# Splitting a block of 640 keys as 384 + 256 columns instead of 512 + 128 in three attention loops

## The chip, the cores and the metric

The kernel runs on one core of one Trainium2 chip. The metric is the device time of one execution in microseconds (us), given as the median of the timed runs. The engines are called as the profile calls them: PE (TensorE, matrix products), PEld (its weight loads), DVE (VectorE), ACT (ScalarE), POOL (GpSimd), SP (the engine that issues most transfers).

## The reference

One layer of a decoder on 1024 positions of width 1024: a half-step SwiGLU, then two attentions side by side that are gated and added, then a second half-step SwiGLU. What matters here are three products with all keys up to a query's own position:

```
# sparse attention: an indexer scores every key, the best 256 are kept
dots  = einsum('bthd,bsd->bths', q_idx, k_idx)          # 8 heads of 64
score = einsum('bths,bth->bts', relu(dots), w_idx)
_, idx = top_k(where(causal, score, -inf), 256)
logits = einsum('bthd,btkd->bthk', q_a, k_a[idx]) * 64 ** -0.5
p = softmax(logits)                                     # then p @ v_a[idx]

# stick-breaking attention, 8 heads of 64
z = einsum('bthd,bshd->bhts', q_b, k_b) * 64 ** -0.5
log_a = log_sigmoid(z) + (reverse cumulative sum of log_sigmoid(-z), strictly causal)
a = exp(log_a)                                          # then a @ v_b
```

All inputs are float32. Queries are handled in 8 blocks of 128; block i may look at the first (i + 1) * 128 keys.

## The kernel before

**Numbers.** Products in full precision are made from parts: an operand is split into a high part in the fast float32 form of PE and the remainder (the low part), and three products (high by high, high by low, low by high) are added up in one accumulator bank; `mm3` at line 310 is that. In the three loops of this change the query's two parts are stacked in the 128 rows of the weight operand, so two products do: one with the high part of the keys, one with the low part.

**The course of the kernel.** The first feed-forward and the projection of the latent queries take up to about 690 us of the profile. Then come two stages in which many small jobs are interleaved by a planner: "index" (queries and keys of the indexer, index scores, and the projections of the second attention as filler work) and "attend" (stick-breaking attention, the threshold of the top 256, sparse attention, more projections and the output products). From about 1410 us on the output projection and the second feed-forward run.

**The planner.** In the two middle stages nothing is left to the scheduler of the language: inside `tc.manual_schedule` (line 1058) the engines run their instructions in the order in which Python writes them. That order is chosen by the class `Weave` (lines 95 to 244). Every job is a generator that yields the engine and the tiles it needs next; `Weave.run` picks, step by step, the job that can begin first by a model of time, and at equal times the one of lower rank. The model gives each instruction a price by engine and width (`cost`, line 113). For PE it is

```
return 0.01 + max(outs[0].free_size(), 240) / 2350, 0.0
```

so the width of a matmul moves the model's clock of PE, and through it every later choice in both stages. `late` and the ranks decide only between jobs that can begin at the same time. The filler jobs on PE (`fillers` at 1232, which writes tiles `psf` and `psvb`, and `outputs` at 2145, which writes `psob` and `psoa`) have the last ranks and take the gaps.

**The three loops.** Each takes the key range of one query block in pieces of at most 512 columns, since one accumulator bank holds 512 float32 values a row. For each piece it takes a bank from one ring of three (`ubank`, line 1091), writes two matmuls and spawns a job that empties the bank.

- `indexer` (line 1681): blocks 5, 4, 2, 7, 6, 3, eight heads each; matmuls at 1695 and 1696 into `psdot`. `dot_out` applies the rectifier on ACT (1665) into one of two tiles `relu` and adds the weighted result to the score `u` on DVE (1670 for the first head, 1672 for the others), head after head for each piece.
- `sticks` (line 1761): for each head blocks 4 to 7, then 0 to 3; matmuls at 1778 and 1779 into `psz`; `sigmoids` on ACT (1753), then one running product over the whole row on DVE (1759).
- `logits` (line 1959): blocks 5, 4, 1, 0, 7, 6, 3, 2, eight heads each; matmuls at 1978 and 1979 into `psL`; `logit_out` on DVE (1938) adds the mask of the selected keys and takes the row's maximum for each piece, `soft` joins the maxima and applies the exponential on ACT.

A last piece of 128 keys is computed as 256 columns (`max(w, 256)` at 1694 and 1774, `max(n_, 256)` at 1976), and the job that empties the bank reads only the first 128 of them. That holds for blocks 0 (128 keys) and 4 (640 keys = 512 + 128).

Of the kernel before, what the change touches and what calls it, by code (L numbers as in the profile page):

```python
# [94 lines left out]
class Weave:  # L95
# [89 lines left out]
    def mark(self, name, *needs):  # L185
        self.marks[name] = needs

    def give(self, *tiles):
        for t in tiles:
            self.held[t.tensor.name] -= 1  # L190
# [19 lines left out]
    def spawn(self, gen, rank=1, own=None):  # L210
        s = Stream(gen, rank, own or self.own)
        self.streams.append(s)
        self.step(s)
        return s
# [33 lines left out]
def trunk(ctx, tc, x, positions, g_ffn1, w1_gate, w1_up, w1_down, g_mix, w_in, g_cq, w_uq_a, w_q_idx,  # L248
# [17 lines left out]
    def ht(name, dt=F32R):  # L266
        return hpool[-1].tile([P, 1024], dt, tag="h", name=name, bufs=16)

    def sm(name, n=1, dt=F32, bufs=4):
        return small.tile([P, n], dt, name=name, bufs=bufs)  # L270
# [39 lines left out]
    def mm3(ps, ah, al, bh, bl, first, last):  # L310

        nc.tensor.matmul(ps, ah, bh, start=first, stop=False)  # L312
        nc.tensor.matmul(ps, ah, bl, start=False, stop=False)  # L313
        nc.tensor.matmul(ps, al, bh, start=False, stop=last)  # L314

    def in_turn(*sources):

        order = [f for n in range(max(n for f, n in sources)) for f, m in sources if n < m]
        at = [0]

        def tile_(name):
            at[0] += 1
            return order[(at[0] - 1) % len(order)](name)

        return tile_
# [59 lines left out]
    class Right:  # L385
# [72 lines left out]
        def keep(self, copies, eng=None):  # L458

            for t, (ps, g) in copies:  # L460
                if eng is nc.vector:
                    nc.vector.tensor_scalar(t, ps, g, None, op0=ALU.mult)
                else:
                    nc.scalar.activation(t, ps, AF.Copy, scale=g)
# [374 lines left out]
    def ring(pool):  # L839

        op = in_turn((wt, 4), (lambda name: pool.tile([P, 1024], F32R, tag="r", name=name, bufs=NR), NR))
        raw = in_turn((rawt, 2), (lambda name: pool.tile([P, 1024], F32, tag="raw", name=name, bufs=2), 2))
        return op, raw
# [7 lines left out]
    with tc.tile_pool(name="ring1", bufs=1) as rpool, tc.tile_pool(name="s1", bufs=1) as spool, tc.tile_pool(name="ps1", bufs=1, space=PSUM) as psum:  # L851
# [3 lines left out]
        with tc.tile_pool(name="t1", bufs=1, side="right") as tpool, tc.tile_pool(name="c1", bufs=1) as cpool:  # L855
# [52 lines left out]
            first = [[load(w, q, f"a{e}r0") for q in range(2)] for e, w in enumerate((w1_gate, w1_up))]  # L908
# [149 lines left out]
    with fp as fpool, psm as psum, tc.manual_schedule(  # L1058
# [157 lines left out]
        def late(rank):  # L1216

            return rank if "sparse" in weave.marks and "gates" not in weave.marks else None
# [442 lines left out]
        def dot_out(ps, i, h, c0, w, acc, before):  # L1661
            yield ACT, ps, relus
            rt = relus("relu")
            r = rt[:, 0:w]
            nc.scalar.activation(r, ps[:, 0:w], AF.Relu)  # L1665
            give(ps)
            yield DVE, rt, before
            wv, ac = WI[:, i, h:h + 1], acc[:, c0:c0 + w]
            if h == 0:
                nc.vector.tensor_scalar(ac, r, wv, None, op0=ALU.mult)  # L1670
            else:
                nc.vector.scalar_tensor_tensor(ac, r, wv, ac, op0=ALU.mult, op1=ALU.add)  # L1672
            give(rt)

        def score_out(i, acc, outs):
            nk = (i + 1) * P
            yield POOL, *outs, acc
            nc.gpsimd.affine_select(acc[:, i * P:nk], acc[:, i * P:nk], pattern=[[-1, P]], compare_op=ALU.is_ge,
                                    fill=LOW, base=0, channel_multiplier=1)

        def indexer():

            for i in order:
                yield PE, "kidx", f"qi{i}"
                nk = (i + 1) * P
                acc = keep(f"u{i}", f"u{i}", 1, shape=(P, nk))
                outs = {}
                for h in range(H):
                    for c0 in range(0, nk, 512):
                        w = min(512, nk - c0)  # L1690
                        yield PE, ubank
                        ps = ubank("psdot")
                        lh = QI[i][:, h * P:(h + 1) * P]
                        x = max(w, 256)
                        nc.tensor.matmul(ps[:, 0:x], lh, KX["h"][:, c0:c0 + x], start=True, stop=False)
                        nc.tensor.matmul(ps[:, 0:x], lh, KX["l"][:, c0:c0 + x], start=False, stop=True)
                        outs[c0] = spawn(dot_out(ps, i, h, c0, w, acc, outs.get(c0)))
                give(QI[i])
                score[i] = acc
                mark(f"score{i}", spawn(score_out(i, acc, list(outs.values()))))  # L1700
# [28 lines left out]
        for n, g in enumerate((latents(), keys(), indexer(), index_queries())):  # L1729
            spawn(g, n)  # L1730
# [20 lines left out]
        def sigmoids(zp, left, c0, w):  # L1751
            yield ACT, zp
            nc.scalar.activation(left[:, c0:c0 + w], zp[:, 0:w], AF.Sigmoid, scale=-1.0)  # L1753
            give(zp)

        def stick(outs, left, nk):
            yield DVE, *outs, left, hidden
            back, ones = left[:, 0:nk][:, ::-1], hidden[:, S - nk:S][:, ::-1]
            nc.vector.tensor_tensor_scan(back, back, ones, 1.0, op0=ALU.mult, op1=ALU.max)  # L1759

        def sticks():

            n, ends = 0, []
            for h, c in work:
                yield PE, f"hq{h}"
                qs, kh, kl = HQ[h]
                for i in range(4 * c, 4 * c + 4):
                    nk = (i + 1) * P
                    yield PE, arings[c]
                    left = arings[c]("left")  # L1770
                    outs = []
                    for c0 in range(0, nk, 512):
                        w = min(512, nk - c0)
                        x = max(w, 256)
                        yield PE, ubank
                        zp = ubank("psz")
                        lq = qs[:, i * P:(i + 1) * P]
                        nc.tensor.matmul(zp[:, 0:x], lq, kh[:, c0:c0 + x], start=True, stop=False)
                        nc.tensor.matmul(zp[:, 0:x], lq, kl[:, c0:c0 + x], start=False, stop=True)
                        outs.append(spawn(sigmoids(zp, left, c0, w)))  # L1780
                    A[n] = left
                    ends.append(spawn(stick(outs, left, nk)))
                    mark(f"s{n}", ends[-1], left)
                    n += 1
                if not c:
                    give(qs, kh, kl)
            mark("sparse", *ends)
# [147 lines left out]
        def logit_out(lp, e, bias, c0, n_, m):  # L1935
            yield DVE, lp
            c = slice(c0, c0 + n_)
            nc.vector.tensor_tensor_reduce(e[:, c], lp[:, 0:n_], bias[:, c], 1.0, LOW, op0=ALU.add, op1=ALU.max,  # L1938
                                           accum_out=m)
            give(lp, bias)  # L1940
# [18 lines left out]
        def logits():  # L1959
            n = 0  # L1960
            yield PE, "sparse", "ka2", "warm"
            kah, kal = KV[:2]
            for b, i in enumerate(blocks):
                nk = (i + 1) * P
                yield PE, f"qa{b}", f"bias{b}"
                QS, bias = QA[b], BIAS[b]
                for h in range(H):
                    rings = [arings[1], lefts] + ([here["e"]] if "e" in here else [])
                    yield PE, rings, late(2)
                    ring = min(rings, key=lambda r: weave.when((r,), PE))  # L1970
                    e, mx, outs = ring("e"), sm("mx", 2, F32, 8), []
                    for g, c0 in enumerate(range(0, nk, 512)):
                        yield PE, ubank, late(2)
                        lp = ubank("psL")
                        n_ = min(512, nk - c0)
                        w = max(n_, 256)
                        lh = QS[:, h * P:(h + 1) * P]
                        nc.tensor.matmul(lp[:, 0:w], lh, kah[:, c0:c0 + w], start=True, stop=False)
                        nc.tensor.matmul(lp[:, 0:w], lh, kal[:, c0:c0 + w], start=False, stop=True)  # L1979
                        outs.append(spawn(logit_out(lp, e, bias, c0, n_, mx[:, g:g + 1])))  # L1980
                    E[n] = e
                    mark(f"p{n}", spawn(soft(n, e, nk, mx, outs)), e)
                    n += 1
                give(QS)
# [182 lines left out]
        first = [feed().parts for n in range(2)]  # L2167
# [6 lines left out]
    with ctxf, tc.tile_pool(name="ring2", bufs=1) as rpool, tc.tile_pool(name="ps6", bufs=1, space=PSUM) as psum:  # L2174
        op, raw = ring(rpool)
        bank = banks(psum, fpsum)
        with tc.tile_pool(name="m0", bufs=1) as mpool:
            M0 = []
            for d in range(0, ND, 2):
                wh, wl = first.pop(0) if first else wcols(w_o_a, d * P, 2 * P, 0, 4, f"woa{d}")  # L2180
                for e in range(2):
                    r = slice((d + e) * P, (d + e + 1) * P)
                    g = ht("gate", F32)
# [150 lines left out]
```

## Time and profile before

| What | Value |
|---|---|
| Median of 3 timed runs | 2137.19 us (2136.37 to 2138.1) |
| Span of the profiled execution | 2135.7 us |
| Busy: PE, PEld, DVE | 2122.0, 1779.9, 1512.9 us |
| Busy: ACT, POOL | 1065.8, 910.1 us |
| Matmuls | 10284 |
| Chain of work that ended last, by engine | PE 93%, DVE 3%, DMA 2%, ACT 1%, issue 1% |

The profile shows one execution; its span runs from the first instruction to the last. Its own time is that span; the median of the timed runs lies 1.5 us above it. A matmul's duration in the rows contains its way through the array, and the next one begins before it ends: what a matmul takes of PE is the distance from its start to the next start.

### The profile page before, as it was taken

The page shows a single profiled execution, that of the slowest core. Times are in us where ns is not written, and L with a number is a line of the kernel's source. Part 1 is how long each engine was busy: PE and PEld are TensorE (multiplying, and loading weights), DVE is VectorE, ACT ScalarE, POOL GpSimd, SP SyncE. Part 2 cuts the span into 40 slices and gives each one's busy share as a digit, 9 for nine tenths or more (in the row PEclk, how much of TensorE's full clock was granted, in tenths as well). Part 3 has the DMA queues.
Part 4 walks back from the last instruction along what each step waited for, and adds up shares of the span by engine and source line. Part 5 has one row for each costly group of instructions (what it writes and reads, how often), then busy time and mean ns, then how long its engine had stood idle before and what let it go on. Part 6 is the DMA issues. An engine that isn't in the chain of part 4 may idle for free.

```text
span 2135.7 us, 30056 instructions
## 1 busy us (share of the span) xinstructions
PE 2122.0 (99%) x10284; PEld 1779.9 (83%) x10284; DVE 1512.9 (71%) x2587; ACT 1065.8 (50%) x2005; POOL 910.1 (43%) x732
## 2 busy tenths in 40 slices
PE   9999999999999999999999999999999999999999
PEld 7888888888889988888888888888888888888887
DVE  7776767688875498898886777754765646578675
ACT  6343343334455357888777686534432222324443
POOL 6654555522355434322311432354664555542233
PEclk9999999999999999999999999999999999999999
DMA  5587867497685342776744534574142333359655
GB/s 149 148 252 212 260 199 239 153 335 245 209 228 165 103 148 85 241 198 163 198 135 162 193 127 149 172 250 142 55 131 92 118 94 117 101 187 333 216 176 188
DMA packets 277578, 377.33 MB, mean 177 GB/s; under 512 B 39840, under 2 KB 165440, under 8 KB 277424
## 3 DMA queue, kind: packets, MB, share of 16 engines
q1 hardware_dynamic: 265392, 337.61, 51.1%
q0 software_dynamic: 12032, 37.79, 4.8%
q8 instruction: 81, 1.33, 0.3%
q14 instruction: 73, 0.60, 0.1%
HBM read 258.38 MB, written 116.95 MB: 176 GB/s over the span
## 4 chain that ended last, share of the span: by engine, by line
PE 93%; DVE 3%; DMA 2%; ACT 1%; issue 1%; POOL 0%; SPq 0%; ACTq 0%; POOLq 0%; DVEq 0%
PE p L769 6%; PE p L770 6%; PE p L768 6%; PE psf L312 4%; PE psf L314 4%; PE psf L313 4%; PE pd L529 3%; PE pd L531 3%; PE pc L529 3%; PE pd L530 3%; PE pa L529 3%; PE pa L531 3%; PE pa L530 3%; PE pc L531 3%; PE pc L530 3%; PE pb L531 2%
## 5 line engine op out<-in xcount | busy, mean ns | idle before, releaser
L1315 ACT ACTIVATE junka<-u,cand,sig 128x768 bf16<-128x768 f32 (+2 forms) x124 | 134.2, 1082 | 3.6 <-DVE cand L1307 2.3
L891 ACT ACTIVATE swh<-swr 128x512 fp32r<-128x512 f32 x48 | 30.2, 630 | 121.4 <-PE pc L531 48.5
L1759 DVE TENSOR_TENSOR_SCAN left<-left,hidden 128x640 f32<-128x640 f32 (+3 forms) x64 | 87.3, 1382 | 0.9 <-ACT left L1753 0.6
L892 DVE TENSOR_TENSOR swr<-swr,swh 128x512 f32<-128x512 f32 x48 | 43.2, 901 | 51.8 <-ACT swh L891 51.7
L672 ACT ACTIVATE b0u<-b0u 128x512 f32<-128x512 f32 x20 | 12.6, 632 | 99.8 <-DVE b0u L552 84.4
L1938 DVE CUSTOM_DVE_ANT_0 e<-psL,bias 128x512 f32<-128x512 f32 (+3 forms) x96 | 49.3, 551 | 16.9 <-PE psL L1979 12.2
L1817 DVE TENSOR_TENSOR pt<-pspT,pt 128x512 fp32r<-128x512 f32 x72 | 46.7, 684 | 18.3 <-ACT pt L1811 18.2
L1814 DVE SCALAR_TENSOR_TENSOR pt<-pstT,pt 128x512 fp32r<-128x512 f32 (+1 forms) x96 | 51.0, 546 | 12.1 <-ACT pt L1811 11.7
L1811 ACT ACTIVATE pt<-pstT 128x512 fp32r<-128x512 f32 (+1 forms) x96 | 46.1, 493 | 22.4 <-PE pstT L1871 19.9
L1950 ACT ACTIVATE e<-e,nm 128x768 f32<-128x768 f32 (+7 forms) x64 | 49.2, 774 | 8.7 <-DVE nm L1945 8.7
L1811 ACT ACTIVATE pt<-pspT 128x512 fp32r<-128x512 f32 x72 | 39.7, 596 | 26.2 <-PE pspT L2033 26.1
L1665 ACT ACTIVATE relu<-psdot 128x512 f32<-128x512 f32 (+1 forms) x80 | 40.5, 520 | 23.9 <-DVE u L1672 13.3
L769 PE MATMUL p<-aT,aS 128*128 128x512 f32 x132 | 51.5, 390 | 0.8 <-DVE aT L382 0.8
L769 PE MATMUL p<-bT,bS 128*128 128x512 f32 x132 | 51.3, 389 | 0.0
L770 PE MATMUL p<-aT,aS 128*128 128x512 f32 x132 | 50.7, 389 | 0.0
L770 PE MATMUL p<-bT,bS 128*128 128x512 f32 x132 | 50.7, 389 | 0.0
L1672 DVE SCALAR_TENSOR_TENSOR u<-relu,WI,u 128x512 f32<-128x512 f32 (+1 forms) x70 | 48.1, 705 | 3.4 <-ACT relu L1665 2.5
L1229 POOL DMA_DIRECT2D gd<-evg x32 | 18.2, 569 | 75.7 <-ACT evg L1224 56.2
L768 PE MATMUL p<-bT,bS 128*128 128x512 f32 x132 | 47.0, 389 | 0.0
L1871 PE MATMUL pstT<-ident,left 128*128 128x128 f32 x288 | 46.0, 272 | 0.0
L768 PE MATMUL p<-aT,aS 128*128 128x512 f32 x132 | 44.9, 389 | 0.0
L381 ACT ACTIVATE bT<-bt 128x512 fp32r<-128x512 f32 x44 | 26.6, 626 | 35.9 <-PE p L770 30.8
(3051 smaller groups left out, 8191.2 us busy)
## 6 DMA issues: line engine op xcount, KB each, us to landing
aw<-in_w_down_dram SPq DMA_DIRECT2D x33, 512.0 KB, 4.6
bw<-in_w_down_dram SPq DMA_DIRECT2D x33, 512.0 KB, 4.6
swr<-in_w_in_dram SPq DMA_DIRECT2D x48, 256.0 KB, 6.1
a0r<-in_w_gate_dram SPq DMA_DIRECT2D x22, 512.0 KB, 8.6
a1r<-in_w_up_dram SPq DMA_DIRECT2D x22, 512.0 KB, 8.5
b0r<-in_w_gate_dram SPq DMA_DIRECT2D x22, 512.0 KB, 4.1
b1r<-in_w_up_dram SPq DMA_DIRECT2D x22, 512.0 KB, 3.9
x<-in_x_dram SPq DMA_DIRECT2D x16, 512.0 KB, 5.9
```

Of the source, the lines that this page charges most:

```text
L312: nc.tensor.matmul(ps, ah, bh, start=first, stop=False)
L313: nc.tensor.matmul(ps, ah, bl, start=False, stop=False)
L314: nc.tensor.matmul(ps, al, bh, start=False, stop=last)
L529: nc.tensor.matmul(ps, a[:, c], b[k][:, HI], start=start and k == 0, stop=False, skip_group_check=True)
L530: nc.tensor.matmul(ps, a[:, c], b[k][:, LO], start=False, stop=False, skip_group_check=True)
L531: ins = nc.tensor.matmul(ps, a[:, l], b[k][:, HI], start=False, stop=k == 3, skip_group_check=True)
L768: nc.tensor.matmul(ps[q][m], S[:, h], T[:, HI], start=p == 0, stop=False)
L769: nc.tensor.matmul(ps[q][m], S[:, h], T[:, LO], start=False, stop=False)
L770: nc.tensor.matmul(ps[q][m], S[:, l], T[:, HI], start=False, stop=p == last)
L1315: nc.scalar.activation(junks[1][:, 0:(i + 1) * P], score[i], AF.Sign, scale=sig[:, b:b + 1], bias=cand.bitcast(F32)[:, b:b + 1], accum_out ...
L1759: nc.vector.tensor_tensor_scan(back, back, ones, 1.0, op0=ALU.mult, op1=ALU.max)
L1811: nc.scalar.activation(pt[:, off:512], tp[:, off:512], AF.Copy, bias=-less)
```

## The change

A new helper cuts a key range into pieces, and the three loops use it in place of `range(0, nk, 512)`:

```
+    def chunks(nk):
+        first = 512 if nk - 512 >= 256 or nk <= 512 else nk - 256
+        return [(c0, min(first, nk) if not c0 else nk - first) for c0 in range(0, nk, first)]
...
-                    for c0 in range(0, nk, 512):
-                        w = min(512, nk - c0)
+                    for c0, w in chunks(nk):
                         yield PE, ubank
                         ps = ubank("psdot")
...
-                    for c0 in range(0, nk, 512):
-                        w = min(512, nk - c0)
+                    for c0, w in chunks(nk):
                         x = max(w, 256)
                         yield PE, ubank
                         zp = ubank("psz")
...
-                    for g, c0 in enumerate(range(0, nk, 512)):
+                    for g, (c0, n_) in enumerate(chunks(nk)):
                         yield PE, ubank, late(2)
                         lp = ubank("psL")
-                        n_ = min(512, nk - c0)
                         w = max(n_, 256)
```

Up to 512 keys there is one piece as before; 768, 896 and 1024 keys give 512 + 256, 512 + 384 and 512 + 512 as before. Only block 4 differs: its 640 keys are 384 + 256 instead of 512 + 128, and the second piece needs no padding: its matmuls cover keys 384 to 639 where they covered 512 to 767. The number of pieces, banks and instructions written for a block stays the same.

## Prediction

> **What bounds the kernel now.** I read the page first: busy time by engine and the granted clock.
>
> ```profile
> span 2135.7 us, 30056 instructions
> ...
> PE 2122.0 (99%) x10284; PEld 1779.9 (83%) x10284; DVE 1512.9 (71%) x2587; ACT 1065.8 (50%) x2005; POOL 910.1 (43%) x732
> ...
> PEclk9999999999999999999999999999999999999999
> ```
>
> PE is busy 99% at a full clock. But that share overlaps the matmuls, so I looked next at the stretches in which the change acts, by the view of windows (columns after the length: busy us and instructions of PE, PEld, DVE, ACT, POOL, then the granted clock and the DMA load). The three later windows are the index stage, stick-breaking with what runs beside it, and sparse attention.
>
> ```profile
> core 0: us, PE busy (x) PEld busy (x) DVE busy (x) ACT busy (x) POOL busy (x), PEclk, DMA share, GB/s
> 10.00:15.00 5.00, 4.72 (x23) 4.25 (x22) 4.34 (x8) 3.14 (x6) 1.83 (x2) 0.50 1.22 294
> 690.00:900.00 210.00, 207.35 (x1221) 182.40 (x1220) 161.90 (x349) 129.96 (x260) 86.54 (x106) 1.00 0.42 140
> 900.00:1150.00 250.00, 249.78 (x1314) 209.93 (x1313) 209.73 (x427) 203.67 (x420) 59.44 (x81) 1.00 0.64 181
> 1150.00:1410.00 260.00, 259.17 (x1358) 218.15 (x1357) 194.91 (x551) 165.47 (x328) 84.23 (x79) 1.00 0.47 155
> ```
>
> PE's idle time is 210 - 207.35 = 2.65 us, 250 - 249.78 = 0.22 us and 260 - 259.17 = 0.83 us: 3.7 us in 720. The second busiest engine, DVE, has 77% (161.9 of 210), 84% (209.7 of 250) and 75% (194.9 of 260). Third, the waits of PE in that stretch (total us, times, longest):
>
> ```profile
> PE psdot L1695 <- ACT relu L1665: 1.4, 3, 1.0
> PE pscqt L1486 <- DMA cqn<-cqd: 1.1, 1, 1.1
> PE psout L313 <- POOL wout000l L301: 0.4, 1, 0.4
> PE pso L2015 <- DVE pt L1817: 0.3, 1, 0.3
> PE psz L1778 <- ACT left L1753: 0.2, 1, 0.2
> ```
>
> These five make 3.4 of the 3.7 us. Of the loops that change, the indexer waits three times for its bank to be emptied by ACT, `sticks` once, `logits` not at all in this list. So in both stages PE is the bound, filler products take the gaps, and a microsecond less on PE is a microsecond less of the stage, as long as the planner's order stays about as good.
>
> **What a column costs on PE.** Last, single starts in the timeline (start, duration). Three neighbouring places give three widths:
>
> ```profile
> 1341.27 0.33 PE L1979 MATMUL psL<-kkl,qs 128*128 128x384 f32 x1
> 1341.44 0.34 PE L1978 MATMUL psL<-kkh,qs 128*128 128x384 f32 x1
> 1341.62 0.34 PE L1979 MATMUL psL<-kkl,qs 128*128 128x384 f32 x1
> 1341.80 0.35 PE L1978 MATMUL psL<-kkh,qs 128*128 128x384 f32 x1
> ```
>
> ```profile
> 1176.71 0.28 PE L1978 MATMUL psL<-kkh,qs 128*128 128x256 f32 x1
> 1176.82 0.28 PE L1979 MATMUL psL<-kkl,qs 128*128 128x256 f32 x1
> 1176.94 0.40 PE L1978 MATMUL psL<-kkh,qs 128*128 128x512 f32 x1
> ...
> 1178.09 0.39 PE L312 MATMUL psf<-mhi,wg6h 128*128 128x512 f32 x1
> ...
> 1179.90 0.39 PE L314 MATMUL psf<-mhi,wg6l 128*128 128x512 f32 x1
> ```
>
> The last two rows are the first and the ninth of nine matmuls of 512 columns in a row: eight distances in 1179.90 - 1178.09 = 1.81 us, 0.226 us each. The 384 columns take (1341.80 - 1341.27) / 3 = 0.177 us, and the 256 columns (1176.94 - 1176.71) / 2 = 0.115 us. The starts are rounded to 0.01 us, so the three-step distance is good to about 0.003 us.
>
> **The change, part by part.** *PE, the only term.* Block 4 alone changes. In each of three loops it has 8 heads, and each head two passes (high and low part of the keys): 3 x 8 x 2 = 48 times a pair of matmuls of 512 + 256 columns becomes one of 384 + 256. The second matmul of the pair keeps its width; it only loses its padding and covers other keys. One matmul per pair goes from 512 to 384 columns: 0.226 - 0.177 = 0.049 us. 48 x 0.049 = 2.35 us, taken as **2.4 us off PE**: 0.8 us each in the indexer, in `sticks` and in `logits`.
>
> The bounds come from other rows for the same step: durations by form (busy us, mean ns), and the weight load that goes with each matmul.
>
> ```profile
> L1696 PE MATMUL psdot<-kil,qsi 128*128 128x512 f32 x48 | 18.9, 393 | 0.0
> L1696 PE MATMUL psdot<-kil,qsi 128*128 128x384 f32 x16 | 5.4, 338 | 0.0
> L1778 PE MATMUL psz<-kkh,qs 128*128 128x512 f32 x48 | 20.1, 419 | 0.0
> L1778 PE MATMUL psz<-kkh,qs 128*128 128x384 f32 x16 | 5.7, 353 | 0.0
> L1979 PE MATMUL psL<-kkl,qs 128*128 128x512 f32 x48 | 18.9, 393 | 0.0
> L1979 PE MATMUL psL<-kkl,qs 128*128 128x384 f32 x16 | 5.4, 338 | 0.0
> L1979 PEld LDWEIGHTS psL<-kkl,qs 128*128 128x128 f32 x96 | 18.2, 189 | 1.7
> ```
>
> The durations shrink by 393 - 338 = 55 ns in the low passes and 419 - 353 = 66 ns in the high pass of `sticks`; 48 x 0.060 = 2.9 us is the upper end. The lower end would be a weight load that sets the pace: 189 ns are more than 177 ns, and 0.226 - 0.189 = 0.037 us a step gives 1.8 us. I take 2.4, since matmuls of 256 columns start 0.115 us apart with the same loads, which therefore lie beside the products.
>
> A page of the Trainium skill speaks for less. "TensorE: Matmul & The Clock Gate", section "Back-to-back issue gap", gives a sustained 81 ns a matmul at 128 columns and 131 ns at 512 where each matmul comes with its own weight load. By that slope 128 columns would be worth an estimated 17 ns, and the change 0.8 us. This trace does not agree: 226 ns at 512 columns in such a stream, with 177 ns at 384 and 115 ns at 256 on one line, and the measurement decides.
>
> *ACT and DVE, which empty the banks.* Before, 512 and 128 columns; after, 384 and 256. The same number of instructions, and all four forms are in the trace:
>
> ```profile
> L1753 ACT ACTIVATE left<-psz 128x512 f32<-128x512 f32 x48 | 28.7, 604 | 0.7 <-PE psz L1779 0.6
> L1753 ACT ACTIVATE left<-psz 128x384 f32<-128x384 f32 x16 | 8.0, 501 | 0.1
> L1753 ACT ACTIVATE left<-psz 128x256 f32<-128x256 f32 x16 | 6.3, 393 | 0.2 <-PE psz L1779 0.2
> L1753 ACT ACTIVATE left<-psz 128x128 f32<-128x128 f32 x16 | 4.5, 279 | 0.0
> L1938 DVE CUSTOM_DVE_ANT_0 e<-psL,bias 128x512 f32<-128x512 f32 x48 | 32.0, 684 | 9.1 <-PE psL L1979 7.6 <-issue 1.5
> L1938 DVE CUSTOM_DVE_ANT_0 e<-psL,bias 128x384 f32<-128x384 f32 x16 | 8.6, 550 | 0.9 <-PE psL L1979 0.9
> L1938 DVE CUSTOM_DVE_ANT_0 e<-psL,bias 128x256 f32<-128x256 f32 x16 | 6.5, 418 | 5.8 <-POOL o L2104 3.2 <-PE psL L1979 2.6
> L1938 DVE CUSTOM_DVE_ANT_0 e<-psL,bias 128x128 f32<-128x128 f32 x16 | 4.2, 284 | 1.0 <-PE psL L1979 1.0
> ```
>
> ACT in `sticks`: 604 + 279 = 883 ns becomes 501 + 393 = 894 ns. DVE in `logits`: 684 + 284 = 968 ns becomes 550 + 418 = 968 ns. Eight heads each: 0.1 us at most, on engines with at least 16% of each stretch free. Taken as nothing; PE's filler products hide it. If that cover were gone, the second bank of a head would come free 393 - 279 = 0.11 us later after its matmul and the first 604 - 501 = 0.10 us earlier: eight times 0.1 us in each loop at worst, 2.4 us over 24 heads, and as likely a gain as a loss.
>
> No transfer is added, dropped or moved past a queue, no wait is added, and the ring of three banks turns as often as before.
>
> *The planner.* Its model prices the narrower matmul at 0.01 + 384 / 2350 = 0.173 us instead of 0.228 us, 0.055 us less, close to the 0.049 us of the trace. So the plan stays as true as it was, but its clock of PE runs ahead from the first head of block 4 in the indexer, and two candidates that were nearly level can swap. From there to the end of sparse attention (about 620 us, over 3000 matmuls) the order may differ in detail, with the same work in it. What changes are the waits where plan and chip part. Bounds from the trace: all 3.7 us of PE's idle time in the stretch can go at best; at worst new ones come, of the size of the largest there is now. Its rows:
>
> ```profile
> 828.09 0.28 PE L314 MATMUL psvb<-wvb11h,mlo 128*128 128x256 f32 x1
> 829.38 0.50 PE L1695 MATMUL psdot<-kih,qsi 128*128 128x512 f32 x1 [1.02 <-ACT relu L1665]
> ```
>
> From start to start that is 1.29 us where a 256-column matmul takes 0.115 us: 1.17 us lost. I take zero for the reordering, between -3.7 us and some +9 us (eight such waits), since I have no reason for either sign.
>
> **Sum.** -2.4 us on a span of 2135.7 us gives 2133.3 us. The median of the timed runs lies 2137.19 - 2135.7 = 1.5 us above the span, and nothing in the change touches that difference: 2137.19 - 2.4 = **2134.8 us**, 0.11% less. About 0.2% (4.3 us) is what a measurement of this kernel can tell from no change, so the forecast is one of no change that can be told.
>
> **Rivals.**
>
> *The reordering also loses waits* (2131 us). All five waits above stem from places where the plan meant the bank, the transfer or the operand to be ready. A new order may miss them: at best 2137.19 - 2.4 - 3.7 = 2131.1 us. For it: the three `psdot` waits lie in the stage where the order first changes, and the first piece's bank is free 0.10 us sooner. Against it: the waits for `pscqt` and `psout` (1.5 us) lie before block 4's first head and after the last of its work, so the change reaches only 2.2 us of the 3.7.
>
> *The reordering adds waits in the index stage* (2144 us, slower). The mechanism: between two heads of the indexer the PE stands in line behind a `psdot` matmul whose bank ACT has not emptied, and ACT waits for a `relu` tile that DVE frees; every filler product is queued behind that matmul and none can pass it. The place is 740 to 860 us. The price is 1.17 us a wait. It decides for "slower" from the sixth new wait on (6 x 1.17 = 7.0, less 2.4 = 4.6 us); eight make 9.4 - 2.4 = 7.0 us, 2144.2 us. For it: idle time is largest there (2.65 of 210 us). Against it: six to eight are many where three are now, ACT and DVE get no more work, and DVE is at 77%. The clock could raise that price: in the window of 10 to 15 us, just after the kernel's first waits, it was granted at 0.50, and five microseconds at half speed are 2.5 us of work lost. The Trainium skill ("TensorE: Matmul & The Clock Gate", section "Why this matters for your kernels") warns of gaps over about 3 us between bursts of matmuls; the largest single wait in the stretch here is 1.17 us, so this trace shows no case of it there.
>
> *The narrower matmul does not free PE* (2137.2 us). If the start of the next product were set by something else than columns, say by its weight load, at most 1.8 us would be left, or nothing. Against it stand the three distances above, which follow the width. By the slope of the Trainium skill quoted above ("TensorE: Matmul & The Clock Gate", "Back-to-back issue gap") the estimate would be 2136.4 us, which lies in this case.
>
> **How the numbers follow.** The forecast has 0.55: the sum holds, with the waits changed by less than 1.9 us either way. Fewer waits have 0.22; I count 0.18 of that beyond 4.3 us of gain, the rest within. More waits have 0.18, of which 0.14 lie over 4.3 us of loss. No effect of the narrower matmul has 0.05. So: faster by over 0.2% 0.18, within 0.2% 0.55 + 0.04 + 0.04 + 0.05 = 0.68, slower by over 0.2% 0.14. The range goes from 2130.8 us (2.9 + 3.5 us of gain: the upper end of the term and nearly all the idle time) to 2141.0 us (five and a half new waits of 1.17 us, less 2.4), and leaves some 0.05 below and 0.12 above it.
>
> **What the profile of the changed kernel would show.** Right: of the rows of 512 columns for `psdot`, `psz` and `psL` 40 instead of 48 are left on each line, 24 instead of 16 of 384 columns; 128-column rows of lines 1665, 1753 and 1938 lose eight and 256-column rows gain eight; the second feed-forward starts, and its first product lies, about 2.4 us earlier, 0.8 us of it in each of the three windows; PE's idle time between 690 and 1410 us stays near 3.7 us. Wrong in the size: consecutive 384-column starts 0.19 us or more apart. Wrong in the planner's part: PE's idle time in that stretch moves by more than 2 us, with new rows among its waits, above all for `psdot`.

## The result, and the profile after

The changed kernel takes 2148.9 us (median of 5 runs, 2147.73 to 2150.88); the kernel before took 2137.74 us beside it (5 runs, 2136.37 to 2141.63). The ratio is 1.0052, with a 95% interval of 1.004 to 1.0064: 11.2 us slower by the medians, where 2.4 us less was forecast.

The page of the changed kernel, with PE's row of the 40 slices (53.7 us each):

```profile
span 2147.1 us, 30062 instructions
...
PE 2121.3 (99%) x10284; PEld 1779.4 (83%) x10284; DVE 1511.8 (70%) x2587; ACT 1064.9 (50%) x2005; POOL 917.9 (43%) x732
...
PE   9999999999999999999999899999999999999999
```

The span grew by 2147.1 - 2135.7 = 11.4 us while PE's busy time fell by 0.7 us. So PE got no more work (POOL shows 7.8 us more for the same 732 instructions, but it is busy for 43% of the span only); PE stands still somewhere, and the slice with the 8 (1181 to 1235 us) says about where. The windows of the three stages narrow it down (same columns as in the prediction):

```profile
690.00:900.00 210.00, 204.79 (x1208) 179.56 (x1206) 162.34 (x339) 125.74 (x252) 88.19 (x106) 1.00 0.44 144
900.00:1150.00 250.00, 249.19 (x1315) 210.71 (x1316) 212.40 (x443) 207.94 (x430) 61.97 (x81) 1.00 0.62 177
1150.00:1410.00 260.00, 250.63 (x1316) 211.31 (x1314) 178.08 (x535) 159.30 (x318) 78.07 (x76) 0.99 0.45 150
```

PE is idle for 5.2, 0.8 and 9.4 us where it was idle for 2.65, 0.22 and 0.83 us, and in the last stage the granted clock is no longer 1.00. PE's waits in this stretch (total us, times, longest) name the place:

```profile
PE pso L2015 <- ACT pt L1814: 8.6, 3, 7.0
PE psz L1781 <- ACT left L1757: 1.7, 1, 1.7
PE pscqt L1491 <- DMA cqn<-cqd: 1.5, 1, 1.5
PE psdot L1699 <- ACT relu L1670: 1.0, 3, 0.5
PE psq L312 <- DVE qy L1631: 0.8, 1, 0.8
```

One wait of 7.0 us is new: `pso`, the product of weights and latent values in sparse attention, waits for ACT's copy `pt` of the transposed weights. PE's timeline there, and then ACT's:

```profile
1207.50 0.34 PE L1981 MATMUL psL<-kkl,qs 128*128 128x384 f32 x1
1214.87 0.79 PE L2015 MATMUL pso<-pt,kkh 128*128 128x512 f32 x1 [7.03 <-ACT pt L1814]
1215.46 0.63 PE L2016 MATMUL pso<-pt,kkl 128*128 128x512 f32 x1
1215.88 0.63 PE L2017 MATMUL pso<-pt,kkh 128*128 128x512 f32 x1
```

```profile
1203.28 1.06 ACT L1814 ACTIVATE pt<-pspT 128x512 fp32r<-128x512 f32 x2
1213.18 1.15 ACT L1918 ACTIVATE uvh<-uvraw 128x512 fp32r<-128x512 f32 x2 [8.84 <-DMA uvraw<-in_w_uv_a_dram]
1214.24 1.06 ACT L1814 ACTIVATE pt<-pspT 128x512 fp32r<-128x512 f32 x2
```

ACT is not busy: it stands 8.84 us in front of two copies `uvh`, the high part of the value projection's weights, whose loads have not landed, and the copies of `pt` that PE needs are queued behind them. Nobody needs `uvh` yet; the first product with it (`psya`) starts at 1248 us. Why the loads are late shows in SP's issues (x4 is four loads in one row):

```profile
1193.72 0.32 SPq L2155 DMA_DIRECT2D yb<-ybhd  x1
...
1204.54 0.32 SPq L2155 DMA_DIRECT2D yb<-ybld  x1
...
1206.53 2.65 SPq L1913 DMA_DIRECT2D uvraw<-in_w_uv_a_dram  x4
```

They leave SP after sixteen loads of `yb`, from 1206.53 us on, 4.6 us after POOL began to clear their tiles (1201.97 us). The larger part of ACT's 8.84 us comes after that: the loads take more than twice as long to land as in the kernel before. The first line is from the chain of work that ended last, the two others are the loads' times from issue to landing in the changed kernel and in the kernel before:

```profile
1207.15 5.92 DMA uvraw<-in_w_uv_a_dram
...
DMA to landing us min/median/max: 4.6/5.7/6.3
...
DMA to landing us min/median/max: 2.0/2.3/2.4
```

The transfer engines are full in these microseconds (share 1.06 from 1207.5 to 1211 us, in the windows further down), with the `yb` loads issued just ahead. So standing behind `yb` makes the loads late twice, on leaving and on landing; that it is the bytes of `yb` that slow the landing is read from that share, and no run separates it.

The planner had meant it otherwise. Its own dates, in its count of us (for `yb` the date at which SP is done with the first load, which the plan takes to land 4.0 us later):

```
                     first yb load   uvraw landed   copies uvh end
kernel before             498.5           527.2      528.6 and 532.0
changed kernel            511.5           514.4      514.7 and 515.2
```

In the new plan the loads of `uvraw` come before those of `yb`, so it writes ACT's copies early. But SP is not among the engines whose order line 1058 of the kernel before holds fixed, and in its queue the loads of `yb` were put first. In the kernel before the plan itself had `yb` first and the copies late. There the loads leave even later, and neither ACT nor PE has a wait for them (SP and ACT there):

```profile
1212.14 2.03 SPq L1910 DMA_DIRECT2D uvraw<-in_w_uv_a_dram  x4
```

```profile
1215.31 0.63 ACT L1915 ACTIVATE uvh<-uvraw 128x512 fp32r<-128x512 f32 x1
1215.97 1.09 ACT L1811 ACTIVATE pt<-pspT 128x512 fp32r<-128x512 f32 x2
```

The wait costs a second time, in the clock. Windows of the changed kernel, for PE alone (busy, granted clock, DMA):

```profile
1207.50:1211.00 3.50, 0.34 (x2) 1.00 1.06 385
1211.00:1215.00 4.00, 0.13 (x1) 0.58 0.35 78
1215.00:1218.00 3.00, 3.00 (x8) 0.50 0.34 116
1218.00:1219.00 1.00, 1.00 (x7) 0.78 0.50 184
```

PE works again from 1214.87 us, but until about 1218.4 us at half the clock: a matmul of 512 columns takes 1215.88 - 1215.46 = 0.42 us instead of 0.226 us. That is about 3.5 x 0.5 = 1.8 us lost.

**Account of the 11.4 us** between the two profiled executions. PE's idle time in the three stages grew by 5.2 + 0.8 + 9.4 - 3.7 = 11.7 us; 7.0 us of that is the one wait. The clock adds 1.8 us, the narrower matmuls take off 2.4 us (the forecast's figure, not measured in this pair): 11.7 + 1.8 - 2.4 = 11.1 us.

### The profile page after: what moved, and what is told of

Its sections match the earlier page's. It is cut to its first block, busy times and chain, and to the rows that moved or that the text cites. A ratio compares the mean times of both kernels' runs of the same rounds, so it can differ in the third digit from the quotient of the medians.

```text
span 2147.1 us, 30062 instructions
## 1 busy us (share of the span) xinstructions
PE 2121.3 (99%) x10284; PEld 1779.4 (83%) x10284; DVE 1511.8 (70%) x2587; ACT 1064.9 (50%) x2005; POOL 917.9 (43%) x732
## 4 chain that ended last, share of the span: by engine, by line
PE 90%; DVE 3%; DMA 3%; ACT 2%; issue 1%; POOL 0%; SPq 0%; ACTq 0%; DVEq 0%; POOLq 0%
PE p L774 6%; PE p L775 6%; PE p L773 6%; PE pd L534 3%; PE pc L534 3%; PE pd L535 3%; PE pd L536 3%; PE pa L534 3%; PE pa L535 3%; PE pa L536 3%; PE pc L535 3%; PE pc L536 3%; PE psf L312 3%; PE psf L314 3%; PE psf L313 3%; PE pb L536 2%
## 5 line engine op out<-in xcount | busy, mean ns | idle before, releaser
L1320 ACT ACTIVATE junka<-u,cand,sig 128x768 bf16<-128x768 f32 (+1 forms) x124 | 134.5, 1084 | 3.8 <-DVE cand L1312 2.5
L1953 ACT ACTIVATE e<-e,nm 128x768 f32<-128x768 f32 (+7 forms) x64 | 49.4, 778 | 15.5 <-DVE nm L1948 15.4
L1677 DVE SCALAR_TENSOR_TENSOR u<-relu,WI,u 128x384 f32<-128x384 f32 (+1 forms) x70 | 50.5, 739 | 3.7 <-ACT relu L1670 3.0
L2106 POOL TENSOR_TENSOR o<-o,gate 128x512 f32<-128x512 f32 x16 | 20.8, 1299 | 63.5 <-ACT o L2101 63.5
```

The source lines that it names most:

```text
L1320: nc.scalar.activation(junks[1][:, 0:(i + 1) * P], score[i], AF.Sign, scale=sig[:, b:b + 1], bias=cand.bitcast(F32)[:, b:b + 1], accum_out ...
```

## The experiments

Theory A: the narrower matmuls do what was forecast, and the loss is the planner's new order. Theory B: the new widths cost something themselves, in the banks or in the work that empties them. Within A: one place carries most of it (A1), or many small waits do (A2). All ratios are to the kernel before on the same chip (medians 2137.63, 2137.81 and 2138.2 us in the three groups), with their 95% intervals; a ratio here is not the quotient of the two medians, from which it differs by up to 0.07%.

**The widths alone.** The changed kernel, with the planner charging block 4 as if nothing had changed:

```
-                cost, late = self.cost(i, eng, outs, ins)
+                cost, late = self.cost(i, eng, outs, ins, ({384: 512, 256: 128}, {384: 512}) if at in self.block4 else None)
```

`block4` holds the instructions that the three loops write for block 4; the first table says at which width ACT and DVE are charged for them, the second at which PE is.

> The changed kernel, with block 4's pieces of 384 + 256 columns priced by the planner as if they were 512 + 128, so that every engine runs its instructions in the order of the kernel before; only the widths differ from it. Theory A (the slowdown is the planner's new order): 48 narrower matmuls take 2.4 us off PE and nothing else moves, 2134 to 2136.5 us, PE's idle time in the two middle stages as before (3.7 us, no wait of several us near 1207 us). Theory B (the widths themselves cost, in the banks or in the work that empties them): 2146 to 2150 us as in the changed kernel.

2136.11 us, ratio 0.9988 (0.9979 to 0.9997): 2.6 us faster, between 0.6 and 4.5; the two medians differ by 1.5 us. The windows and the head of the list of waits, from one of its faster executions (2133.84 us):

```profile
690.00:900.00 210.00, 207.30 (x1220) 182.53 (x1218) 163.66 (x354) 131.31 (x262) 86.01 (x106) 1.00 0.42 140
900.00:1150.00 250.00, 249.62 (x1316) 210.17 (x1315) 210.19 (x428) 203.01 (x419) 60.55 (x81) 1.00 0.64 179
1150.00:1410.00 260.00, 259.32 (x1364) 219.19 (x1363) 192.96 (x547) 166.86 (x328) 89.11 (x80) 1.00 0.47 156
```

```profile
PE psdot L1712 <- ACT relu L1681: 1.7, 3, 1.0
PE pscqt L1501 <- DMA cqn<-cqd: 0.9, 1, 0.9
PE pso L2034 <- DVE pt L1835: 0.5, 1, 0.5
```

PE is idle for 2.7 + 0.4 + 0.7 = 3.8 us, as before (3.7). Theory B falls: with the old order the new widths cost nothing, and the gain has the forecast size, as far as so wide an interval can say. This version also beats both kernels.

**The order alone.** The counterpart: the kernel before, 512 + 128 columns, with block 4 charged as 384 + 256.

```
+                cost, late = self.cost(i, eng, outs, ins, ({512: 384, 128: 256}, {512: 384}) if at in self.block4 else None)
```

> The kernel before, with 512 + 128 columns, but with block 4's pieces priced as 384 + 256, so that every engine has the order of the changed kernel. Theory A (order): the changed kernel's time plus the 2.4 us that the wider matmuls cost, 2149.5 to 2153 us, with the wait of some 7 us of PE for the transposed weights near 1207 us. Theory B (widths): 2136 to 2139 us as before.

2148.63 us, ratio 1.005 (1.0037 to 1.0063), with a wait of 7.3 us of PE for `pt` and a clock of 0.68 in the window 1214 to 1220 us:

```profile
PE pso L2030 <- ACT pt L1826: 8.9, 3, 7.3
...
1214.00:1220.00 6.00, 5.86 (x20) 4.33 (x21) 4.98 (x18) 2.70 (x6) 1.58 (x2) 0.68 0.29 89
```

The slowdown is there without one changed width. The extra 2.4 us that this order should still cost with the wider matmuls are not seen: it came out 0.9 us under the expected range. Both ratios are known to 0.13% (2.7 us), so 2.5 us between them cannot be settled. In the two profiled executions PE is idle for 15.4 us in the three stages with the narrower matmuls and for 13.3 us with the wider ones, which would take up 2.1 of the 2.4 us.

**One date.** The changed kernel, the two copies held back in the plan:

```
+            weave.flush()
+            for raw in raws:
+                weave.ready[raw.tensor.name] += 14.0
             for half, raw in enumerate(raws):
                 cols = slice(half * 512, half * 512 + 512)
                 yield ACT, raw
```

> The changed kernel, with one planner date moved: the two raw tiles of the value projection count as landed 14 us later, so that ACT's two copies of them are written after the copies of transposed weights that PE waits for. Theory A1 (most of the loss is this one place: ACT stands 8.8 us in front of the copy, behind it PE 7.2 us, and then PE runs at a lowered clock): 7.2 us of wait and about 2 us of clock are gone, 2138 to 2141 us, clock 1.00 in all of 1200 to 1230 us. Theory A2 (the loss is spread over many small waits of the new order, and others take the place of this one): 2145 us or more.

2138.96 us, ratio 1.0003 (0.9994 to 1.0012). PE's and DVE's orders stay those of the changed kernel; ACT's differs in where the two copies stand, and a few rows of POOL and SP move with them. The windows (PE, PEld, DVE, ACT, POOL, clock, DMA) at the place:

```profile
1208.00:1214.00 6.00, 5.89 (x31) 4.51 (x30) 5.96 (x26) 3.27 (x8) 0.00 (x0) 1.00 0.90 291
1214.00:1220.00 6.00, 5.17 (x28) 3.88 (x27) 5.16 (x22) 5.97 (x14) 1.06 (x3) 1.00 0.29 87
```

PE works, the clock stays at 1.00. From 1.0052 to 1.0003 is 0.49%, 10.5 us, good to some 3 us: A1 carries nearly all of the 11 us, and A2 what may be left. Against the old order with the same widths (0.9988) this one still costs 0.15%, some 3 us; that these are small waits is an inference from the list of waits, whose longest is one of 1.1 us.

**The same place from the other side.** If the copies may stay early but the loads come early too, the wait should go as well:

```
-                    nc.sync.dma_start(f32(yb[half, p][:, part]), ...)
+                    tc.keep_in_program_order(nc.sync.dma_start(f32(yb[half, p][:, part]), ...))
...
-                    nc.sync.dma_start(raw.rearrange(...), w_uv_a[...])
+                    tc.keep_in_program_order(nc.sync.dma_start(raw.rearrange(...), w_uv_a[...]))
```

> The changed kernel; on SP's queue the four loads of the value projection's raw weights stand ahead of the sixteen loads of yb instead of behind them (both are kept in the order in which the program writes them). PE, DVE, ACT and POOL keep the changed kernel's order to the instruction. Theory A1a (ACT's copy stands early in its queue and waits for loads that SP issues late): the loads can leave once POOL has cleared their tiles near 1203 us and land by about 1206 us, the 8.8 us of ACT and the 7.2 us of PE behind them go, the clock stays at 1.00: 2138 to 2142 us. Theory A1b (the 16 loads of yb are what fills the transfer engines, and pushing them back by 10 us makes PE wait for yb instead): 2144 to 2150 us, with a wait of several us before psob.

2140.13 us, ratio 1.0013 (1.0004 to 1.0021). The loads leave SP from 1199.9 us on, 0.6 us after POOL began to clear their tiles (1199.3 us) where it was 4.6 us, they land after 3.4 to 4.1 us instead of 4.6 to 6.3, ACT waits a third as long, and PE's wait for `pt` shrinks to 1.3 us at the longest:

```profile
1204.59 1.32 ACT L1918 ACTIVATE uvh<-uvraw 128x512 fp32r<-128x512 f32 x2 [2.92 <-DMA uvraw<-in_w_uv_a_dram]
1205.82 1.07 ACT L1814 ACTIVATE pt<-pspT 128x512 fp32r<-128x512 f32 x2
```

Only SP's order differs from the changed kernel, so the cause of the long wait is the pair: a copy early in ACT's queue, and its loads late in SP's.

**One loop at a time.** In each of three kernels one loop uses `chunks(nk)` and the two others keep `range(0, nk, 512)`.

> The change in the indexer alone; stick-breaking and sparse logits keep 512 + 128. 0.8 us less on PE. Theory A (order): what it does beyond that is the order; its written order differs from the kernel before by about as much as the changed kernel's, but the value projection's loads stand behind five of the yb loads instead of all sixteen, so no wait of several us: 2135 to 2142 us. Theory C (the indexer's part alone carries the loss, whatever the later order): 2147 us.

2139.11 us, ratio 1.0004 (0.9995 to 1.0012).

> The change in the stick-breaking logits alone. 0.8 us less on PE. Theory A (order): the value projection's loads stand behind all loads of yb, and ACT's two copies of them stand about four instructions after the second copy of sparse results, earlier than in the kernel before (seven and ten) and later than in the changed kernel (before that copy): a shorter wait of 0 to 5 us of PE there, 2136 to 2143 us. Theory C' (this part alone carries the loss): 2147 us.

2139.64 us, ratio 1.0007 (0.9999 to 1.0016).

> The change in the sparse logits alone. 0.8 us less on PE; the order changes only from about 1150 us on and least of the three; ACT's two copies for the value projection stand eight instructions after the second copy of sparse results, as in the kernel before: 2135 to 2138 us by theory A. Theory C'' (this part alone carries the loss): 2147 us.

2142.52 us, ratio 1.0023 (1.0013 to 1.0033), above the range expected. No part alone carries the loss, and the parts do not add up to the whole (0.04 + 0.07 + 0.23 = 0.34% against 0.52%): each is another order. None has the long wait. `logits_only` changes the order least; its longest wait of PE is one of 1.7 us for `cqn`, ahead of all changes, and the next one of 1.4 us for `pt` at 1323 us. Its twelve executions also scatter most, from 2139.7 us at a mean granted clock of 0.999 to 2150.63 us at 0.997, so one program can lose a different time from one execution to the next, and a profile shows one of them.

**Nudging the planner.** Is this change special, or does any nudge of the planner's clock move the time? The kernel before, with the delay between engines at 0.151 instead of 0.150 us:

```
-    HOP = 0.15
+    HOP = 0.151
```

> The kernel before with its own widths; the planner's delay between engines is 0.151 instead of 0.150 us, nothing else. The order differs from the kernel before by about as much as one loop's change makes. Theory A3 (any nudge of the planner's clock throws the times by several us, in either direction): outside 2135.5 to 2140 us, between 2130 and 2150. Theory A4 (orders are mostly equal in worth and this change hit one bad place): 2136 to 2140 us.

2142.16 us, ratio 1.0019 (1.001 to 1.0028): 4 us slower, for a number that no instruction contains. That is outside A4's range, as A3 has it; that a nudge can also gain, the other half of A3, was not seen.

The same edit in the changed kernel, with three values chosen for where the two copies stand in the written order:

> The changed kernel with the planner's delay between engines at 0.151 instead of 0.150 us. In its written order ACT's first copy of the value projection stands ahead of the copy of transposed weights that the second result of sparse attention still needs, and its loads stand behind all sixteen loads of yb, as in the changed kernel. If that arrangement is what costs (theory A1): 2146 to 2151 us, ACT 7 to 10 us in front of that copy near 1204 us, PE 6 to 8 us behind it, clock at 0.50 after that. If it is some other feature of the changed kernel's order (theory A5): anywhere from 2135 to 2146 us without that wait.

2148.76 us, ratio 1.0044 (1.0031 to 1.0058): ACT waits 10.4 us for `uvraw`, PE 8.6 us behind it, both a little longer than expected. As A1 has it; but this written order is the changed kernel's up to that place and beyond (PE's first differs at its 6183rd of 10284 matmuls), so it repeats the case more than it tests another.

> The changed kernel with the planner's delay at 0.146 us; both copies of the value projection stand behind the second result of sparse attention with copies of transposed weights between them, as in the kernel before. Theory A1: 2134 to 2142 us, no wait of over 2 us in the two middle stages. Theory A5: 2146 us or more.

2140.24 us, ratio 1.0009 (1.0 to 1.0018), no wait over 1.6 us. As A1 has it.

> The changed kernel with the planner's delay at 0.152 us. In its written order both copies of the value projection stand behind the second result of sparse attention, the loads behind the yb loads as before. Theory A1: no long wait of PE at that place, or one hidden by PE's other work, 2135 to 2142 us, which is 2.5 us less than an order of equal worth would give with 512 + 128 columns. Theory A5: 2146 us or more.

2148.5 us, ratio 1.0041 (1.0029 to 1.0054): a miss of A1, at the time that A5 gives. The wait behind `uvh` is gone, as read from the order, but two others are there (PE's waits):

```profile
PE psvb L313 <- POOL wvb11l L1125: 3.1, 1, 3.1
PE pspT L2035 <- ACT e L1958: 1.9, 1, 1.9
```

At 819 us PE reaches a filler product before POOL has made its low weights, because POOL ran a small power function first that took 2.10 us there; at 1205 us it waits for a scaled row. Each is followed by a spell at half clock (the second below). Neither is a feature of the changed kernel, which has no wait for `wvb11l` and one of 0.3 us for `pspT`, so A5 is not borne out. The bad arrangement is enough for a time near 2148 us, but it is not the only one that gives it. Windows of 1 us around the second wait, for PE alone:

```profile
1206.00:1207.00 1.00, 0.00 (x0) 1.00 0.96 352
...
1209.00:1210.00 1.00, 1.00 (x3) 0.62 1.05 399
1210.00:1211.00 1.00, 1.00 (x5) 0.50 1.06 393
...
1213.00:1214.00 1.00, 1.00 (x5) 1.00 1.06 416
```

## Why the prediction was wrong

**PE's term held**, as far as it could be measured. -2.4 us were forecast; with the order kept, the same widths gave -2.6 us (-4.5 to -0.6). The rows of 512 and 384 columns changed as said, 48 to 40 and 16 to 24 on each line:

```profile
L1981 PE MATMUL psL<-kkl,qs 128*128 128x512 f32 x40 | 15.7, 392 | 0.0
L1981 PE MATMUL psL<-kkl,qs 128*128 128x384 f32 x24 | 8.2, 341 | 0.0
```

The rival by which the narrower matmul frees nothing lies outside that interval, its other form (1.8 us, paced by weight loads) inside it. Starts in the changed kernel follow the width as before: 1207.50 - 1207.32 = 0.18 us between two matmuls of 384 columns in its timeline. The 0.8 us by the slope in the Trainium skill ("TensorE: Matmul & The Clock Gate", "Back-to-back issue gap") lie just inside the interval, so the starts speak against that slope here and the time alone does not.

**The eviction term held**: ACT and DVE gained no work (1064.9 after 1065.8 us, 1511.8 after 1512.9 us), and with the old order PE's idle time stayed at 3.8 us.

**The step that failed is the planner's**: "I take zero for the reordering, between -3.7 us and some +9 us (eight such waits), since I have no reason for either sign." The term was put at 0 and measured 10.7 us (7.9 to 13.5, by `wide_new_order`, where nothing but the order changed). There was a reason for a sign, and it stands in the bounds themselves: the order before leaves PE idle for 3.7 us in 720, so a new order could take off almost nothing and add waits. Nothing holds plan and chip together either, since SP's queue isn't bound by the plan. Ten other orders were run, of both widths; with PE's term taken out (0.11%, or 0.04% for one loop) the measured ratio of every one lies above the old order's, from about 0.1% to 0.6%, the smallest of them within their intervals. They are no fair sample, since three share most of the changed kernel's order and three were picked by where two copies stand.

**The bound on a new wait was taken from the wrong rows.** By "at worst new ones come, of the size of the largest there is now" I sized it at 1.17 us, and so asked for six of them. (The range's upper end has a slip besides: 5.5 x 1.17 - 2.4 = 4.0 us give 2141.2 us, not 2141.0.) What decides is how long the engine ahead of PE can stand, in a queue that nothing passes: ACT stood for 8.84 us in front of a transfer, and one such wait was enough. The rows for it were in the trace before: an `uvh` copy that only the plan's date keeps behind its loads, and sixteen `yb` loads of 0.26 MB each ahead of them in SP's queue. "No transfer is added, dropped or moved past a queue, no wait is added" was true of the edited lines and not of the order that they cause: the copy moved ahead of its loads' landing.

**The rival on the slower side had the right sign, too small a total and the wrong place.** It gave 2144 us by eight short waits for `psdot` in the index stage. The chip gave 2148.9 us, with one long wait for `pt` in sparse attention; the `psdot` waits fell from 1.4 to 1.0 us. The sign of error that the prediction had set, PE's idle time moving by more than 2 us, came (3.7 to 15.4 us), but not with `psdot` in front.

**The clock** was dismissed because "this trace shows no case of it there". The page of the Trainium skill named in that place, "TensorE: Matmul & The Clock Gate" ("Why this matters for your kernels"), warned of gaps over about 3 us, and this trace agrees: 7.0 us of wait, then 0.50 of the clock. It made that wait a quarter dearer (1.8 us on 7.0).

**What stays open**: what the narrower matmuls are worth inside the new order (the two kernels with it differ by less than their intervals); which waits make up the last 3 us there; and why SP's queue took the loads of `yb` first.

## What to carry to other kernels

Where a planner or a list scheduler turns prices into an order, a change of a price is a change of the whole order from there on, and its effect can be several times that of the work saved (here 10.7 us against 2.4): forecast the two apart, and measure them apart by keeping the old prices for the new instructions. A stall of the bound engine is sized by what stands ahead of its supplier in a strict queue: look for copies of just-loaded data that nobody needs yet, written ahead of work that somebody does. Where the bound engine is idle for half a percent, as in this kernel's middle stages, a new order has little to win, so the risk of reordering is mostly on one side.

## What the runs showed of the hardware

In the changed kernel the half clock began some 4 us into the 7.0 us wait (1.00 until 1211 us) and lasted into 3.5 us of work. In `after_hop151` it began 2.4 us into the wait of 8.6 us that starts at 1207.04 us (0.70 in the window 1209 to 1210 us). It also came after shorter waits, both in `after_hop152`: 3.1 us at 819 us (0.50 from 824 to 826 us), and 1.9 us at 1205 us, there from about 1209.2 us on, when PE had been at work again for 2 us. For 3.4 us around that last wait, from 1204.77 to 1208.17 us, PE ran nothing but transposes.

The Trainium skill ("TensorE: Matmul & The Clock Gate", "Part 4: PE-mode transpose") says that transposes do not count as busy in the same way. By that the 3.4 us would be one gap. But each of the 13 traces has three stretches of 3.5 to 4.1 us with nothing but 32 transposes between ordinary products, and the clock stays at 1.00 in and after all of them. One from the kernel before, its row and PE's windows there and behind it:

```profile
33.14 3.65 PE L443 MATMUL pst<-ident,x 128*128 128x128 f32 x32
...
33.14:37.37 4.23, 3.65 (x33) 1.00 0.09 25
37.37:41.00 3.63, 3.63 (x16) 1.00 0.39 116
```

So transposes alone did not bring the half clock here, and why a wait of 1.9 us among them did once stays open.
